# The last eight gate blocks of a hybrid attention block as seven block products for eight

## The chip, the cores and the metric

The kernel runs on one core of one Trainium2 chip. The metric is the device time of one execution in microseconds; the time before is the median of three runs. Engines: PE (TensorE, matmuls; PEld are its weight loads), DVE (VectorE), ACT (ScalarE), POOL (GpSimd), and SP (SyncE), which issues most DMAs. Each engine works through its own list of instructions in order and waits where an operand is not ready or a buffer is not free.

## The reference

One layer of a residual block with two attention branches, batch 1, sequence and model width 1024, all in float32. What matters here are the gates: the last 2048 columns of the input projection.

```python
h = rms_norm(x, g_pre_mix[l])
proj = h @ w_in[l]                      # 1024 x 5120
c0 = 3 * SB_WIDTH
c1 = c0 + 3 * DIFF_WIDTH
sb_q, sb_k, sb_v = jnp.split(proj[..., :c0], 3, axis=-1)
d_q, d_k, d_v = jnp.split(proj[..., c0:c1], 3, axis=-1)
gates = jax.nn.sigmoid(proj[..., c1:])
gate_sb, gate_diff = jnp.split(gates, N_BRANCHES, axis=-1)
y_sb = stick_breaking_attention(...)     # 8 heads of 64
y_diff = differential_attention(...)     # 4 heads, two softmax maps each
merged = gate_sb * (y_sb @ w_sb_out[l]) + gate_diff * (y_diff @ w_diff_out[l])
x = x + rms_norm(merged @ w_o[l], g_post_mix[l])
h = rms_norm(x, g_pre_mlp[l])
u = jnp.square(jax.nn.relu(h @ w_up[l]))
x = x + rms_norm(u @ w_down[l], g_post_mlp[l])
```

## The kernel before

Every product is taken in three float32r matmuls: each operand is split into a high part (a cast on ACT) and the rest (a subtraction on DVE), and high x high, high x low and low x high are added in one PSUM bank. `load_split` (L95 to L104) does this for a weight block: a DMA into a tile with tag raw (two buffers), the cast (L102), the subtraction (L103).

h, transposed, lies in eight tiles `h_hi[k]` and eight `h_lo[k]` of 128 x 1024: k counts 128 rows of the model width, the columns are the sequence. A gate block b (`gate`, L453, through `project`, L189) is 128 columns of the projection: for each half of the sequence it adds 24 matmuls of 128x512 (L196 to L198: eight k, three each) in a bank with tag acc, which has two; ACT copies the sum out (L456) and SP stores it in `gate_dram`. Gates are only needed by the next stage, mix (L542 to L582), where g is loaded back, passed through the sigmoid and multiplied.

The attention runs in eight units: four of two stick-breaking heads, then four differential heads. A unit's steps (j = 3, 1, 2, 0, a pair of query tiles each) go: scores z (PE L262, L263, in the two banks of tag sc), bias added and the row minimum found (DVE L389), exponential (ACT L394), the combination of the two maps (DVE L400 to L404), transposes (PE L281), their split (ACT L287, DVE L288), the products with v (PE L342 to L344), and a normalisation that goes back and forth between ACT, DVE and PE (L348 to L368, with ss on PE at L355 and L356). The steps of the last head, called head 3 below, begin when its bias rows have been loaded (L372); there is one bias buffer. Score tiles have the tags big_s (four buffers, j = 3 and 2) and small_s (four buffers, j = 1 and 0).

Gates 0 to 7 are written between the units' steps (`GATES`, `fill`). Gates 8 to 15 are written in a plain loop behind the last step (L530 to L532), but the order of the instructions on each engine is not the written one: a scheduler (the tile framework's, with a timeline of its own) lays them out when the kernel is built, with buffers of a tag handed on as they come free. It put much of these eight gates between the steps of heads 2 and 3.

The MLP behind it already uses seven block products for eight: `sums` (L724) forms sums of weight blocks on POOL, L817 to L830 form sums of h on DVE.

Of the kernel before, what the change touches and what calls it, by code (L numbers as in the profile page):

```python
# [9 lines left out]
F32 = mybir.dt.float32  # L10
F32R = mybir.dt.float32r
AF = mybir.ActivationFunctionType
ALU = mybir.AluOpType
# [3 lines left out]
P = 128  # L17
S = 1024
D = 1024
NK = D // P  # L20
NT = S // P
HALF = 512
# [19 lines left out]
def hybrid_block_kernel(  # L42
# [17 lines left out]
    nc = tc.nc  # L60
# [20 lines left out]
    def f32(ap):  # L81
        return ap.bitcast(F32)
# [46 lines left out]
    gate_dram = dram.tile([2 * NK, P, S], F32, name="gate_dram")  # L129
# [20 lines left out]
    with ExitStack() as actx:  # L150
        pa = actx.enter_context(tc.tile_pool(name="pa", bufs=2))

        h_hi = [big_tile(f"h_hi{k}") for k in range(NK)]
        h_lo = [big_tile(f"h_lo{k}") for k in range(NK)]
# [337 lines left out]
        qs, kh, kl, pair = [], [], [], []  # L492
# [34 lines left out]
            for _ in filler:  # L527
                pass
        waiting()
        for b in range(GATES[-1].stop, 2 * NK):  # L530
            for _ in gate(b):
                pass  # L532


        def load_gate(b, i):
# [7 lines left out]
        for u in range(N_SB + N_DIFF):  # L543
            if u < 6:
                tag = ("qs", "kh", "kl")[u % 3]
                parts = [pa.tile([P, S], F32R, tag=tag, name=f"y{u}_{p}", bufs=4) for p in range(2)]
            else:
                both = pa.tile([P, 2, S], F32R, tag="v", name=f"y{u}", bufs=3)
# [8 lines left out]
        for b in range(NK):  # L557
            w_hi, w_lo = load_split(w_mix[b], f"mix{b}")
            g = [load_gate(b, i) for i in range(2)]
            accs = [[any_tile(f"mix{b}_{i}_{c}") for c in range(2)] for i in range(2)]  # L560
            for k in range(NK):
                i, ks = k // 4, slice(k * P, (k + 1) * P)
                y_hi, y_lo = y[k]
                for st, mv, first, last in ((w_hi, y_hi, True, False), (w_hi, y_lo, False, False), (w_lo, y_hi, False, True)):
                    for c in range(2):
                        cs = slice(c * HALF, (c + 1) * HALF)
                        nc.tensor.matmul(  # L567
                            accs[i][c], st[:, ks], mv[:, cs],
                            start=(first and k % 4 == 0), stop=(last and k % 4 == 3),
                        )  # L570
            for c in range(2):
                cs = slice(c * HALF, (c + 1) * HALF)
# [178 lines left out]
    for t in range(NT):  # L751
# [337 lines left out]
```

## Time and profile before

| | us |
|---|---|
| median of three runs | 1463.02 (1461.43 to 1464.18) |
| the profiled execution | 1462.9 |
| its span, first to last instruction | 1461.2 |
| attention units, last gates among them, until the last gate matmul | to 653.5 |
| mix starts | 653.75 |
| DVE busy / ACT busy / POOL busy, of the span | 1018.6 / 742.9 / 320.6 |

Spans of one execution are read against the 1462.9, which lies 0.1 from the median. A line such as `0.69 DVE L389` is a start, a duration, an engine and a line of the kernel; what stands in square brackets is the idle time ahead of it and what ended it. Instructions on PE overlap: one 128x512 matmul lasts 0.39 us and the next starts 0.23 us after it.

### The profile page before, as it was taken

What the parts mean: (1) busy time and instruction counts of PE and PEld (TensorE: products, weight loads), DVE (VectorE), ACT (ScalarE), POOL (GpSimd) and SP (SyncE); (2) the same over time, 40 slices, a digit from 0 to 9 for tenths busy, and PEclk for the clock granted to TensorE, in tenths of its full rate; (3) what the DMA queues carried; (4) which work ended last, traced back from release to release, by engine and by line L of the source; (5) the groups of instructions that cost most, each with busy time, mean ns of one, the idle gap of its engine ahead of it and who ended that gap; (6) DMA issues with size and microseconds to landing.
All of it is one profiled execution on the core that took longest, in us unless ns stands there. A gap on an engine that the chain in (4) does not pass through costs nothing. (4 is left out here: it accounts for less than half of the span.)

```text
span 1461.2 us, 20068 instructions
## 1 busy us (share of the span) xinstructions
PE 1437.1 (98%) x7302; PEld 1221.7 (84%) x7302; DVE 1018.6 (70%) x1468; ACT 742.9 (51%) x1352; POOL 320.6 (22%) x312
## 2 busy tenths in 40 slices
PE   7999999999999999999999989999999999999997
PEld 6888898899889888888888868788888888888886
DVE  5477987898779876535555489766665669764783
ACT  6355766676556645753434454444444443534350
POOL 2022331231000000000002316333330357232611
PEclk9999999999999999999999999999999999999999
DMA  5242213221322245554347735544446785678681
GB/s 206 76 135 66 69 48 80 65 73 48 93 74 66 80 130 170 179 197 139 138 149 238 245 117 178 189 148 143 152 158 202 256 287 178 200 229 285 205 288 58
DMA packets 93946, 220.50 MB, mean 151 GB/s; under 512 B 9260, under 2 KB 24856, under 8 KB 93848
## 3 DMA queue, kind: packets, MB, share of 16 engines
q1 hardware_dynamic: 79448, 199.30, 42.5%
q10 hardware_dynamic: 14400, 19.93, 3.8%
q8 instruction: 57, 0.93, 0.3%
q14 instruction: 41, 0.34, 0.1%
HBM read 153.11 MB, written 60.05 MB: 146 GB/s over the span
## 5 line engine op out<-in xcount | busy, mean ns | idle before, releaser
L331 DVE TENSOR_TENSOR_SCAN rest<-rest 128x896 f32<-128x896 f32 (+3 forms) x64 | 87.7, 1374 | 20.7 <-POOL rest L326 20.3
L198 PE MATMUL acc_gate<-h_hi,lo_gate 128*128 128x512 f32 x256 | 101.0, 394 | 0.0
L196 PE MATMUL acc_gate<-h_hi,hi_gate 128*128 128x512 f32 x256 | 100.8, 394 | 0.0
L197 PE MATMUL acc_gate<-h_lo,hi_gate 128*128 128x512 f32 x256 | 100.7, 394 | 0.0
L608 DVE TENSOR_TENSOR lS_lo<-raw_S,lS_hi 128x1024 fp32r<-128x1024 f32 x32 | 53.8, 1680 | 39.8 <-ACT lS_hi L607 39.8
L326 POOL TENSOR_SCALAR_AFFINE_SELECT rest<-rest 128x128 f32<-128x128 f32 x64 | 23.6, 369 | 240.7 <-ACT rest L322 228.0
L957 PE MATMUL dS<-rT_hi,lS_hi 128*128 128x512 f32 x192 | 74.7, 389 | 0.0
L957 PE MATMUL dS<-rT_lo,lS_hi 128*128 128x512 f32 x192 | 74.7, 389 | 0.0
L957 PE MATMUL dS<-rT_hi,lS_lo 128*128 128x512 f32 x192 | 74.7, 389 | 0.0
L607 ACT CAST lS_hi<-raw_S 128x1024 fp32r<-128x1024 f32 x32 | 33.7, 1053 | 73.9 <-DMA raw_S<-s_dramS 43.5
L567 PE MATMUL mix<-y,hi_mix 128*128 128x512 f32 x256 | 68.6, 389 | 0.0
L394 ACT ACTIVATE s<-s,low 128x896 f32<-128x896 f32 (+7 forms) x64 | 49.7, 777 | 30.1 <-DVE low L389 29.9
L389 DVE CUSTOM_DVE_ANT_0 s<-z,bias 128x512 f32<-128x512 f32 (+3 forms) x64 | 37.0, 588 | 32.3 <-PE z L263 26.1
L567 PEld LDWEIGHTS mix<-y,hi_mix 128*128 128x128 f32 x256 | 48.1, 188 | 10.0
L198 PEld LDWEIGHTS acc_gate<-h_hi,lo_gate 128*128 128x128 f32 x256 | 48.2, 188 | 9.2
L197 PEld LDWEIGHTS acc_gate<-h_lo,hi_gate 128*128 128x128 f32 x256 | 48.2, 188 | 8.8
L196 PEld LDWEIGHTS acc_gate<-h_hi,hi_gate 128*128 128x128 f32 x256 | 48.2, 188 | 8.6
L326 POOL TENSOR_SCALAR_AFFINE_SELECT beta<-beta 128x128 f32<-128x128 f32 x64 | 54.0, 844 | 3.4 <-ACT beta L323 2.3
L287 ACT CAST wth_sb<-tr_sb 128x512 fp32r<-128x512 f32 (+1 forms) x80 | 41.2, 548 | 26.5 <-PE tr_sb L281 25.1
L116 POOL TENSOR_SCALAR rstd_o<-s 128x1 f32<-128x1 f32 x8 | 2.7, 342 | 235.8 <-DMA grow<-in_g_rows_dram 211.4
L288 DVE TENSOR_TENSOR wtl_sb<-tr_sb,wth_sb 128x512 fp32r<-128x512 f32 (+1 forms) x80 | 48.5, 628 | 7.7 <-ACT wth_sb L287 7.4
L322 ACT ACTIVATE rest<-z 128x512 f32<-128x512 f32 (+2 forms) x96 | 47.3, 492 | 9.2 <-PE z L263 7.8
(351 smaller groups left out, 4763.2 us busy)
## 6 DMA issues: line engine op xcount, KB each, us to landing
s_dramS<-us SPq DMA_DIRECT2D x64, 256.0 KB, 4.2
raw_S<-s_dramS SPq DMA_DIRECT2D x32, 512.0 KB, 4.5
s_dramA<-u ACTq DMA_DIRECT2D x48, 256.0 KB, 3.1
raw_A<-s_dramA SPq DMA_DIRECT2D x24, 512.0 KB, 4.1
raw_gate<-in_w_in_dram SPq DMA_DIRECT2D x16, 512.0 KB, 3.7
gate_dram<-gt SPq DMA_DIRECT2D x32, 256.0 KB, 2.5
y<-y_dram SPq DMA_DIRECT2D x16, 512.0 KB, 7.2
g<-gate_dram SPq DMA_DIRECT2D x16, 512.0 KB, 4.3
```

Of the source, the lines that this page charges most:

```text
L196: nc.tensor.matmul(acc, w_hi[:, ks], h_hi[k][:, cs], start=(k == 0), stop=False)
L197: nc.tensor.matmul(acc, w_hi[:, ks], h_lo[k][:, cs], start=False, stop=False)
L198: nc.tensor.matmul(acc, w_lo[:, ks], h_hi[k][:, cs], start=False, stop=(k == NK - 1))
L287: nc.scalar.copy(hi[:, :n], tr[:, :n])
L288: nc.vector.tensor_tensor(lo[:, :n], tr[:, :n], f32(hi[:, :n]), op=ALU.subtract)
L322: nc.scalar.activation(rest[:, c0:c1], z, AF.Sigmoid, scale=-1.0)
L326: nc.gpsimd.affine_select(tl[:, dg], tl[:, dg], pattern=[[-1, P]], compare_op=ALU.is_gt, fill=fill, base=0, channel_multiplier=1,)
L331: nc.vector.tensor_tensor_scan(back, back, back, 1.0, op0=ALU.mult, op1=ALU.bypass)
L394: e = nc.scalar.activation(s[:, :nk], s[:, :nk], AF.Exp, bias=low, scale=-1.0, accum_out=sums[:, m:m + 1],)
L567: nc.tensor.matmul(accs[i][c], st[:, ks], mv[:, cs], start=(first and k % 4 == 0), stop=(last and k % 4 == 3),)
L608: nc.vector.tensor_tensor(lo, raw, f32(hi), op=ALU.subtract)
L957: nc.tensor.matmul(acc, st[:, e, ts], mv[:, e, :], start=(first and e == 0 and i == 0), stop=(last and e == 1 and i == 2))
```

## The change

The loop over the last eight gates (8 to 15) is replaced. The gates go in four pairs (b0, b1). For a pair, the weights A (two column blocks by two halves of the model width) and h as four quarters B (half of the model width by half of the sequence, four k each) make a product of two by two blocks, which is done in seven block products of 12 matmuls each:

- B11, B22 and B21 are products with a quarter of h as it is. First all four pairs' B11, then B22, then B21. The factor of B22 is a sum of the pair's four weight blocks, formed by three sums on POOL (`gate_sums(n, 1)`); the others take a half block as loaded. The results of B11 and B22 are kept in four buffers of tag big_s.
- T1, T2, T3 and T4 are sums of quarters of h. They are formed on DVE, nine instructions and a cast for each of four k, into tiles of the attention's tags (v, qs, kl, yt) and then written over the quarters (T1 over B11's, T2 over B22's, T4 over B21's, T3 over B12's), each when the products that read the quarter are done.
- The last sixteen products take these. Per pair: P6 with T2, P5 with T1, P7 with T3, P4 with T4, in banks of tags sc, av, tr and acc. Their weights are loaded again, two sums of them are formed on POOL (three instructions, `gate_sums(n, 2)`), four splits follow, and six additions on DVE make the four results.

All raw loads go through the same two raw buffers as before.

```diff
-        for b in range(GATES[-1].stop, 2 * NK):
-            for _ in gate(b):
-                pass
+        C0, C1 = slice(0, HALF), slice(HALF, S)
+        gate_pairs = [(b, b + 1) for b in range(GATES[-1].stop, 2 * NK, 2)]
+        def quarter(j, cs):
+            return [(h_hi[4 * j + k][:, cs], h_lo[4 * j + k][:, cs]) for k in range(4)]
+        quarters = {"T1": quarter(0, C0), "T3": quarter(0, C1), "T4": quarter(1, C0), "T2": quarter(1, C1)}
+        PLACE = {"B11": "T1", "B12": "T3", "B21": "T4", "B22": "T2"}
+        def gate_product(acc, w, name):
+            w_hi, w_lo = w
+            for k, (hi, lo) in enumerate(quarters[PLACE.get(name, name)]):
+                ks = slice(k * P, (k + 1) * P)
+                for i, (st, mv) in enumerate(((w_hi, hi), (w_hi, lo), (w_lo, hi))):
+                    nc.tensor.matmul(acc, st[:, ks], mv, start=(k == 0 and i == 0), stop=(k == 3 and i == 2))
+        def split_w(src, name):
+            both = stream.tile([P, 2, HALF], F32R, tag="w", name=f"gw_{name}", bufs=4)
+            nc.scalar.copy(both[:, 0, :], src)
+            nc.vector.tensor_tensor(both[:, 1, :], src, f32(both[:, 0, :]), op=ALU.subtract)
+            return both[:, 0, :], both[:, 1, :]
+        def raw_gate(b, cs, name):
+            raw = stream.tile([P, S], F32, tag="raw", name=f"raw_{name}")
+            nc.sync.dma_start(out=raw[:, cs], in_=w_in[GATE + b][:, cs])
+            return raw
+        def gate_sums(n, part):
+            f0, f1 = (raw_gate(b, slice(0, S), f"g{part}_{b}") for b in gate_pairs[n])
+            a11, a12, a21, a22 = (f[:, cs] for f in (f0, f1) for cs in (C0, C1))
+            s1 = pa.tile([P, HALF], F32, tag="small_s", name=f"gs1_{part}_{n}", bufs=4)
+            nc.gpsimd.tensor_tensor(s1, a21, a22, op=ALU.add)
+            if part == 2:
+                nc.gpsimd.tensor_tensor(a21, a11, a21, op=ALU.subtract)
+            nc.gpsimd.tensor_tensor(a11, s1, a11, op=ALU.subtract)
+            if part == 1:
+                nc.gpsimd.tensor_tensor(a12, a12, a11, op=ALU.subtract)
+            return s1, f0, f1
...
+        t1 = pa.tile([P, 4, HALF], F32, tag="v", name="gt1", bufs=3)
+        t2, t4 = ([pa.tile([P, 2, HALF], F32, tag=tag, name=f"g{tag}{i}", bufs=4) for i in range(2)] for tag in ("qs", "kl"))
+        for k in range(4):
+            (a_hi, a_lo), (b_hi, b_lo), (c_hi, c_lo), (d_hi, d_lo) = (quarters[t][k] for t in ("T1", "T3", "T4", "T2"))
+            t1k, t2k, t4k = t1[:, k, :], t2[k // 2][:, k % 2, :], t4[k // 2][:, k % 2, :]
+            r = pa.tile([P, HALF], F32, tag="yt", name=f"gr_{k}")
+            nc.vector.tensor_tensor(r, f32(b_hi), f32(b_lo), op=ALU.add)
+            nc.vector.tensor_tensor(t1k, r, f32(a_hi), op=ALU.subtract)
+            nc.vector.tensor_tensor(t1k, t1k, f32(a_lo), op=ALU.subtract)
+            nc.vector.tensor_tensor(t2k, f32(d_hi), f32(d_lo), op=ALU.add)
+            nc.vector.tensor_tensor(r, t2k, r, op=ALU.subtract)
+            nc.scalar.copy(b_hi, r)
+            nc.vector.tensor_tensor(b_lo, r, f32(b_hi), op=ALU.subtract)
+            nc.vector.tensor_tensor(t2k, t2k, t1k, op=ALU.subtract)
+            nc.vector.tensor_tensor(t4k, f32(c_hi), t2k, op=ALU.subtract)
+            nc.vector.tensor_tensor(t4k, t4k, f32(c_lo), op=ALU.add)
+        p1s, p3s = ([pa.tile([P, 2, HALF], F32, tag="big_s", name=f"gp{p}_{i}", bufs=4) for i in range(2)] for p in (1, 3))
...
+        for name, cs in (("B11", C0), ("B22", C1), ("B21", C1)):
+            for n, (b0, b1) in enumerate(gate_pairs):
+                if name == "B22":
+                    src = gate_sums(n, 1)[1]
+                else:
+                    src = raw_gate(b0, cs, f"g{name}_{b0}")
+                acc = acc_tile(f"gate_{name}_{n}")
+                gate_product(acc, split_w(src[:, cs], f"{name}_{n}"), name)
...
+            where, tiles = {"B11": ("T1", None), "B22": ("T2", t2), "B21": ("T4", t4)}[name]
+            for k, (hi, lo) in enumerate(quarters[where]):
+                src = t1[:, k, :] if tiles is None else tiles[k // 2][:, k % 2, :]
+                nc.scalar.copy(hi, src)
+                nc.vector.tensor_tensor(lo, src, f32(hi), op=ALU.subtract)
+        for n, (b0, b1) in enumerate(gate_pairs):
+            s1, f0, f1 = gate_sums(n, 2)
+            w2 = split_w(f0[:, C0], f"s2_{n}")
...
+            gate_product(p6, w2, "T2")
+            nc.vector.tensor_tensor(p1, p6, p1, op=ALU.add)
+            gate_product(p5, w1, "T1")
...
+            gate_product(p7, w3, "T3")
...
+            gate_product(p4, w22, "T4")
```

The scheduler lays out the whole again. Three places show what became of the order; the numbers in names are buffers or counters, z are scores, tr transposes, avd products with v, ss the sum of squares, acc_gate and gate_B the gates' banks, gw their split weights, raw_g the pairs' weights as loaded.

PE, behind the second score tiles of head 3, before:

```order
L262 MATMUL z_0_7_0_6542<-kh_dfk_0_5974,qs_dfq_0_5908 128x512
L263 MATMUL z_0_7_0_6542<-kl_dfk_0_5976,qs_dfq_0_5908 128x512
L198 MATMUL acc_gate_0_7051<-h_hi_162,lo_gate_7048 128x512
L196 MATMUL acc_gate_1_7079<-h_hi_155,hi_gate_7047 128x512
L262 MATMUL z_0_7_512_6547<-kh_dfk_0_5974,qs_dfq_0_5908 128x512
L263 MATMUL z_0_7_512_6547<-kl_dfk_0_5976,qs_dfq_0_5908 128x512
L197 MATMUL acc_gate_1_7079<-h_lo_163,hi_gate_7047 128x512
L198 MATMUL acc_gate_1_7079<-h_hi_155,lo_gate_7048 128x512
L196 MATMUL acc_gate_1_7079<-h_hi_156,hi_gate_7047 128x512
L197 MATMUL acc_gate_1_7079<-h_lo_164,hi_gate_7047 128x512
```

PE at the same place in the changed kernel:

```order
L262 MATMUL z_0_7_0_6542<-kh_dfk_0_5974,qs_dfq_0_5908 128x512
L263 MATMUL z_0_7_0_6542<-kl_dfk_0_5976,qs_dfq_0_5908 128x512
L356 MATMUL ss_2_6494<-sqp_2_6491,ones 128x256
L262 MATMUL z_0_7_512_6547<-kh_dfk_0_5974,qs_dfq_0_5908 128x512
L263 MATMUL z_0_7_512_6547<-kl_dfk_0_5976,qs_dfq_0_5908 128x512
L262 MATMUL z_1_7_0_6554<-kh_dfk_1_5975,qs_dfq_1_5909 128x512
L263 MATMUL z_1_7_0_6554<-kl_dfk_1_5977,qs_dfq_1_5909 128x512
L262 MATMUL z_1_7_512_6559<-kh_dfk_1_5975,qs_dfq_1_5909 128x512
L263 MATMUL z_1_7_512_6559<-kl_dfk_1_5977,qs_dfq_1_5909 128x512
L262 MATMUL z_0_2_0_6609<-kh_dfk_0_5974,qs_dfq_0_5908 128x384
```

Where gate matmuls lay between the scores, one score now stands behind the other: two B11 products come earlier, the other products later.

DVE, the end of head 3's last normalisation, before:

```order
L361 TENSOR_TENSOR sq_0_6961<-sq_0_6961,r_0_6962 128x256
L362 SCALAR_TENSOR_TENSOR w_0_6963<-sq_0_6961,r_0_6962 128x256
L363 SCALAR_TENSOR_TENSOR w_0_6963<-w_0_6963,r_0_6962 128x256
L364 SCALAR_TENSOR_TENSOR y_0_6960<-y_0_6960,subln,w_0_6963 128x256
L367 TENSOR_TENSOR yp_0_6979<-y_0_6960,yp_0_6979 128x256
L103 TENSOR_TENSOR lo_mix_7590<-raw_mix_7587,hi_mix_7589 128x1024
L578 TENSOR_TENSOR g_0_7515<-mix_0_0_7521,g_0_7515 128x512
```

DVE at the same place in the changed kernel (gr, gt and gqs are the sums of h; gw_B_2 is the split for the third B22 product):

```order
L362 SCALAR_TENSOR_TENSOR w_0_6963<-sq_0_6961,r_0_6962 128x256
L551 TENSOR_TENSOR gw_B_2_7179<-raw_g_12_7170,gw_B_2_7179 128x512
L363 SCALAR_TENSOR_TENSOR w_0_6963<-w_0_6963,r_0_6962 128x256
L364 SCALAR_TENSOR_TENSOR y_0_6960<-y_0_6960,subln,w_0_6963 128x256
L581 TENSOR_TENSOR gr_6988<-h_hi_155,h_lo_163 128x512
L367 TENSOR_TENSOR yp_0_6979<-y_0_6960,yp_0_6979 128x256
L582 TENSOR_TENSOR gt_6983<-gr_6988,h_hi_155 128x512
L583 TENSOR_TENSOR gt_6983<-gt_6983,h_lo_163 128x512
L585 TENSOR_TENSOR gr_6988<-gqs_6984,gr_6988 128x512
L588 TENSOR_TENSOR gqs_6984<-gqs_6984,gt_6983 128x512
```

The first two of the B22 splits stand ahead of this piece, the third in it, the fourth some ten rows behind it; the sums of h, but for four of the 36, and all twelve rewrites follow the attention, where mix followed.

SP, the loads around head 3's bias, before:

```order
L98 DMA raw_gate_7169<-in_w_in_dram 128x1024
L551 DMA y_0_7483<-y_dram_79 128x1024
L551 DMA y_0_7479<-y_dram_78 128x1024
L551 DMA y_1_7480<-y_dram_78 128x1024
L551 DMA y_1_7484<-y_dram_79 128x1024
L372 DMA bias_6508<-bias_rows 128x1024
L551 DMA y_0_7487<-y_dram_80 128x1024
L551 DMA y_1_7488<-y_dram_80 128x1024
```

SP at the same place in the changed kernel (y are the attention's results, loaded for mix; raw_g_10 and raw_g_11 the weights of the second pair):

```order
L556 DMA raw_g_8_7120<-in_w_in_dram 128x1024
L556 DMA raw_g_9_7122<-in_w_in_dram 128x1024
L658 DMA y_0_7656<-y_dram_79 128x1024
L658 DMA y_1_7657<-y_dram_79 128x1024
L372 DMA bias_6508<-bias_rows 128x1024
L368 DMA y_dram_84<-yp_1_6308 256x1x256
L368 DMA y_dram_84<-yp_2_6504 256x1x256
L368 DMA y_dram_84<-yp_0_6603 256x1x256
L658 DMA y_0_7668<-y_dram_82 128x1024
L658 DMA y_0_7652<-y_dram_78 128x1024
L658 DMA y_1_7669<-y_dram_82 128x1024
L658 DMA y_1_7653<-y_dram_78 128x1024
```

Ahead of the bias two gate loads and two y loads now stand in place of one gate load and four y loads; the next row is the load of raw_g_10, behind four y loads.

More of the change, by code (lines that the diff above doesn't have):

```diff
@@ new lines, in store_gate @@
+        def store_gate(b, cs, tile_):
+            nc.sync.dma_start(out=gate_dram[b, :, cs], in_=tile_)
+        t1 = pa.tile([P, 4, HALF], F32, tag="v", name="gt1", bufs=3)
[14 more added lines that the diff above has]
+            nc.vector.tensor_tensor(t4k, t4k, f32(c_lo), op=ALU.add)
@@ new lines, in hybrid_block_kernel, with kept @@
+        p1s, p3s = ([pa.tile([P, 2, HALF], F32, tag="big_s", name=f"gp{p}_{i}", bufs=4) for i in range(2)] for p in (1, 3))
+        def kept(tiles, n):
+            return tiles[n // 2][:, n % 2, :]
+        for name, cs in (("B11", C0), ("B22", C1), ("B21", C1)):
[6 more added lines that the diff above has]
+                gate_product(acc, split_w(src[:, cs], f"{name}_{n}"), name)
+                if name == "B21":
+                    c11 = pa.tile([P, HALF], F32, tag="small_s", name=f"gc11_{n}", bufs=4)
+                    nc.vector.tensor_tensor(c11, acc, kept(p1s, n), op=ALU.add)
+                    store_gate(b0, C0, c11)
+                else:
+                    nc.scalar.copy(kept(p1s if name == "B11" else p3s, n), acc)
+            where, tiles = {"B11": ("T1", None), "B22": ("T2", t2), "B21": ("T4", t4)}[name]
[3 more added lines that the diff above has]
+                nc.vector.tensor_tensor(lo, src, f32(hi), op=ALU.subtract)
```

15 lines of the change are left out of this document (added).

## The prediction

> **What bounds the kernel now.** I read the page's busy shares first, then the stretch that the change touches: busy time in windows, the matmul timeline at its end, VectorE's timeline at its beginning. The columns of a window row are its length, then PE, PEld, DVE, ACT and POOL busy time with instruction counts, the granted clock, the DMA share and GB/s.
>
> ```profile
> span 1461.2 us, 20068 instructions
> PE 1437.1 (98%) x7302; PEld 1221.7 (84%) x7302; DVE 1018.6 (70%) x1468; ACT 742.9 (51%) x1352; POOL 320.6 (22%) x312
> ...
> 540.00:560.00 20.00, 20.00 (x108) 17.10 (x107) 9.78 (x30) 9.42 (x25) 0.15 (x1) 1.00 0.76 250
> 560.00:580.00 20.00, 20.00 (x96) 16.73 (x95) 17.23 (x44) 11.10 (x24) 0.00 (x0) 1.00 0.35 119
> ...
> 640.00:660.00 20.00, 20.00 (x91) 16.57 (x90) 6.60 (x12) 7.84 (x11) 0.00 (x0) 1.00 0.54 185
> ...
> 555.40:653.60 98.20, 98.20 (x498) 83.22 (x497) 56.18 (x140) 63.06 (x113) 0.12 (x1) 1.00 0.50 165
> ...
> 653.52 0.39 PE L198 MATMUL acc_gate<-h_hi,lo_gate 128*128 128x512 f32 x1
> 653.75 0.84 PE L567 MATMUL mix<-y,hi_mix 128*128 128x512 f32 x3
> ```
>
> PE has no idle time at all from 540 us to the last gate matmul at 653.52 us; the next stage (mix) starts at 653.75. But it is full only because the last eight gates, which need nothing from the attention, are laid between the attention's short matmuls. VectorE, at 56.18 of 98.20 us, shows the room there is. The last head (head 3 of the differential attention) starts when its bias has landed:
>
> ```profile
> 555.37 0.69 DVE L389 CUSTOM_DVE_ANT_0 s<-z,bias 128x512 f32<-128x512 f32 x1 [5.93 <-DMA bias<-bias_rows]
> ...
> 612.50 0.42 DVE L389 CUSTOM_DVE_ANT_0 s<-z,bias 128x256 f32<-128x256 f32 x1 [0.48 <-PE z L263]
> ```
>
> VectorE sat 5.93 us for that load, and reached the last scores of the head at 612.50. PE covered both with gates. So the question is not what a product costs but whether PE still has something to do while VectorE works.
>
> **The change, part by part.** Prices of single instructions:
>
> ```profile
> 939.43 2.72 PE c L781 x12
> ...
> 667.32 0.68 DVE L580 TENSOR_TENSOR g<-g,g 128x512 f32<-128x512 f32 x1
> 667.92 1.46 DVE L582 TENSOR_TENSOR m_lo<-g,m_hi 128x512 fp32r<-128x512 f32 x2
> ...
> L581 ACT CAST m_hi<-g 128x512 fp32r<-128x512 f32 x10 | 6.2, 624 | 10.1 <-DVE g L580 10.1
> ...
> L735 POOL TENSOR_TENSOR s<-up x8: 1285/1290/1890, 866.7 to 1087.5; 128x512 f32<-128x512 f32 x8
> ...
> raw_gate<-in_w_in_dram SPq DMA_DIRECT2D x16, 512.0 KB, 3.7
> ...
> y<-y_dram SPq DMA_DIRECT2D x16, 512.0 KB, 7.2
> ...
> L103 DVE TENSOR_TENSOR lo_gate<-raw_gate,hi_gate 128x1024 fp32r<-128x1024 f32 x6 | 7.3, 1222 | 4.3 <-ACT hi_gate L102 4.3
> ...
> L103 DVE TENSOR_TENSOR lo_mix<-raw_mix,hi_mix 128x1024 fp32r<-128x1024 f32 x1 | 1.2, 1227 | 0.5 <-ACT hi_mix L102 0.5
> ...
> L361 DVE TENSOR_TENSOR sq<-sq,r 128x256 f32<-128x256 f32 x6 | 2.5, 424 | 7.0 <-ACT r L360 7.0
> ```
>
> A product of 12 matmuls takes PE 2.72 us. VectorE starts the next instruction 0.60 us after a 128x512 one (667.32 to 667.92). A 128x512 cast is 0.62 on ACT, a 128x512 sum 1.29 on POOL, a 512 KB gate load lands in 3.7.
>
> Removed: 32 products become 28, so 48 matmuls or 4 x 2.72 = 10.9 us of PE. Also eight wide splits (1.22 on VectorE each) and 16 evictions on ACT, which no chain waits for.
>
> Added: 104 instructions of 128x512 on VectorE (28 splits of weights, 36 sums of h, 12 rewrites of its quarters, 28 combinations; the order has 96 rows more, eight wide splits being gone): 104 x 0.60 = 62 us against 8 x 1.22 = 10 us. 24 sums on POOL, 31 us on an engine that idles here; 17 more DMAs on SP. On ACT casts take the place of evictions; it was busy 63.06 of 98.20 us, and only its casts ahead of splits lie on a chain. None of this is long for its engine over the whole kernel. What matters is where it stands.
>
> Step 1, head 3 without cover. By the order, PE had 201 gate matmuls between head 3's first and last scores, and 361 from its first scores to the end of the gates; now it has 24 between those scores. The first two B11 products are spent before head 3; the other two wait for score tiles to come free (their kept results go into tag big_s). So while the bias lands PE stands (no loss in itself, since VectorE waits for the same load at the same time: I cost the start at nothing, with 3 us either way for the two 512 KB loads that now go ahead of it in place of two others), and then VectorE sets the pace. Its attention work after 555.4 is 56.18 less the splits, 7.3 + 1.2: 47.7 us. Two late normalisations of seven instructions at 0.42 (5.9 us) come afterwards, so 41.8 us plus some 1.5 of waits (estimate): the head's main part is over at about 598.7, where VectorE does the first B22 split. That is sooner than before, and PE idles for most of it.
>
> Step 2, the B22 rounds. The four B22 products need a load, three sums on POOL, a cast and a split, in two raw buffers. The next pair's load can only start when the last split has freed its buffer: 3.7 + 3 x 1.29 + 0.62 + 0.60 + 0.4 for the hand-overs = 9.2 us a round, against 2.72 us of product. On SP the second pair's load also stands behind four y loads, which wait for head 3's last scores and take 7.2 to land: from about 592 that gives the same 603 as the buffer does. So splits at 598.7, 607.9, 617.1, 626.3. They stand in VectorE's queue ahead of, and among, the sums of h, so VectorE waits with them: the late normalisations and twelve sums fit between, no more.
>
> Step 3, the sums of h. After the fourth B22 split the order has 37 more VectorE instructions before the first product of the last set (P5) has all it needs: 37 x 0.60 = 22.2, 648.5. PE has four B21 products (10.9 us) to do meanwhile and idles for the rest.
>
> Step 4, the last sixteen products: 16 x 2.72 = 43.5, less 1.4 for the six matmuls sent ahead, plus 0.5 of waits: 691.1. Their loads and sums (9.2 us) fit under the 10.9 us that a pair takes, ten VectorE instructions (6 us) too, so PE sets the pace.
>
> Step 5, the clock. What an idle PE costs afterwards is shown where the MLP starts:
>
> ```profile
> 844.70:847.80 3.10, 0.47 (x3) 0.04 (x1) 2.26 (x3) 0.00 (x0) 0.00 (x0) 0.99 0.06 25
> 847.80:849.40 1.60, 1.56 (x8) 1.59 (x9) 1.60 (x3) 0.00 (x0) 0.00 (x0) 0.50 0.52 105
> 849.40:851.30 1.90, 1.90 (x7) 1.57 (x6) 1.86 (x4) 0.97 (x2) 0.00 (x0) 0.54 0.70 226
> 851.30:853.30 2.00, 2.00 (x10) 1.62 (x9) 2.00 (x4) 2.00 (x6) 0.00 (x0) 1.00 0.62 229
> ```
>
> After 2.6 us without a matmul the granted clock is 0.50 to 0.54 for 3.5 us, then 1.00 again: half of 3.5, or 1.7 us, when the last products start. 692.8.
>
> The Trainium skill (TensorE: Matmul & The Clock Gate, What's actually happening) has the PE clock at half after an idle window of about 3.4 us and back after as long of sustained work. The trace agrees on the size of the penalty, and shows it after a shorter gap.
>
> The sum: mix starts at 692.8 instead of 653.75, 39 us later; behind it nothing is changed. The profiled execution took 1462.9 (1.7 around its span of 1461.2), the median of the three runs is 1463.0: 1502.
>
> **The rivals.**
> - VectorE never waits (1488). If the rounds hide wholly, VectorE needs 47.7 + 53 x 0.60 = 79.5 us from 555.4 until P5: 634.9, then 42.6 and 1.7: mix at 679.2, 25 us later. This is the floor of this order. For it: the first pair's loads stand ready early, and VectorE may fall behind the rounds by itself; against it, the 9.2 us of a round, three times.
> - Head 3 keeps its old pace (1522). Its last scores then come at 612.5 instead of about 592, and the rounds, whose y loads wait for them, move by 20. POOL's sums at their maximum of 1.89 would add 3 x 3 x 0.6 = 5 to the forecast, which also lies inside. For it: ACT and VectorE alternate in each step; against: then each score matmul stood among gates.
> - Half clock throughout (1514). If PE stays cold in the starved stretch, head 3's 16 pairs of score matmuls (0.46 each at full clock) and as much again of transposes and products with v take twice as long on VectorE's chain, some 12 to 15 us with little cover: 12 taken. The clock rule cited above would give this, if gaps come often enough.
> - Faster (1452). All of the added work is hidden and 10.9 us are won. The point from which it decides: after 555.4 PE has 98.2 - 361 x 0.227 = 16 us of attention and 120 matmuls (27 us) of early products, so it runs dry at 599; to win anything, P5 must start within 10.9 us of that, by 610. VectorE has 47.7 us of attention to do by then, so the 53 instructions before P5 would have to cost 0.13 us each and not 0.60.
> - No change needs the same at 0.2 to 0.25 us each.
>
> **How the numbers follow.** Forecast 0.56, VectorE's floor 0.18, old pace 0.10, half clock 0.08, faster 0.06, no change 0.02. Within 0.2%, some 3 us, is what the runs can tell from no change. So slower 0.92, same 0.02, faster 0.06. The range goes from the floor less the 3 us of the bias load, 1485, to the old pace and 2 us of slower sums, 1524.
>
> **What would show it.** Right: PE idle of 40 us or more between 549 and 690 in the windows, where there was none; VectorE over 80% busy from 556 to 600; the B22 splits about 9 us apart, waiting for a cast that waits for POOL, whose first sum waits for a load; granted clock near 0.5 in pieces; P5 releasing at about 648 on VectorE; the last sixteen products in 43 us; mix at about 693, and everything after it as long as before. Wrong: PE without gaps in 556 to 600 would mean that the products were available after all; splits 5 us apart, that the raw buffers are not the bound; a mix start before 679, that my price of 0.60 or the order's count is off.

## The result, and the profile after

The changed kernel takes 1516.1 us (median; 1514.0 to 1518.2) against 1462.8 for the kernel before on the same chip: 53.3 us more, ratio 1.0356, 95% interval 1.0339 to 1.0373. The forecast was 1502, range 1485 to 1524. The direction came as forecast, and PE starves at the places that were named; the loss is 14 us larger than the sum.

The profiled execution took 1518.15 (its span 1516.4). It is 3.7 us late already at the first scores of the differential heads (354.1 instead of 350.4), ahead of anything that the change moves; head 3's wait for its bias takes that back (1.67 us of it instead of 5.93). Mix starts at 710.79 instead of 653.75, 57.0 us later (one matmul of mix stood at 648.09 before). Some 2 us come back behind mix.

The first two lines of the page, and the stretch in windows (columns as above): from the first idle of PE to the end of head 3's main part, to the point where the first of the last products has its operands, and to the last of them.

```profile
span 1516.4 us, 20192 instructions
PE 1453.5 (96%) x7254; PEld 1225.1 (81%) x7254; DVE 1090.8 (72%) x1564; ACT 741.1 (49%) x1369; POOL 353.0 (23%) x336
...
549.00:600.00 51.00, 38.34 (x187) 29.75 (x187) 44.00 (x125) 28.71 (x71) 4.06 (x4) 0.82 0.28 96
600.00:661.00 61.00, 38.06 (x133) 28.23 (x132) 51.50 (x77) 23.70 (x47) 17.28 (x12) 0.75 0.56 183
661.00:711.00 50.00, 45.52 (x190) 36.09 (x189) 30.99 (x43) 12.87 (x18) 12.55 (x9) 0.97 0.55 175
```

PE, which had no idle time here, now has 12.7, 22.9 and 4.5 us of it, 40 in all, and works at a mean granted clock of 0.82 and 0.75 in the first two pieces. VectorE is busy 86% of the first and 84% of the second.

The B22 rounds, as VectorE's splits, and as the first of POOL's three sums in each round, with what POOL waited for:

```profile
600.05 0.68 DVE L551 TENSOR_TENSOR gw_B<-raw_g,gw_B 128x512 fp32r<-128x512 f32 x1
611.07 0.69 DVE L551 TENSOR_TENSOR gw_B<-raw_g,gw_B 128x512 fp32r<-128x512 f32 x1
622.93 0.69 DVE L551 TENSOR_TENSOR gw_B<-raw_g,gw_B 128x512 fp32r<-128x512 f32 x1
635.43 0.68 DVE L551 TENSOR_TENSOR gw_B<-raw_g,gw_B 128x512 fp32r<-128x512 f32 x1
...
594.19 1.26 POOL L563 TENSOR_TENSOR gs<-raw_g 128x512 f32<-128x512 f32 x1 [38.22 <-DVE s L404]
604.44 1.40 POOL L563 TENSOR_TENSOR gs<-raw_g 128x512 f32<-128x512 f32 x1 [6.18 <-DMA raw_g<-in_w_in_dram]
615.51 1.53 POOL L563 TENSOR_TENSOR gs<-raw_g 128x512 f32<-128x512 f32 x1 [6.87 <-DMA raw_g<-in_w_in_dram]
...
682.07 1.29 POOL L563 TENSOR_TENSOR gs<-raw_g 128x512 f32<-128x512 f32 x1 [9.02 <-DMA raw_g<-in_w_in_dram]
696.95 1.26 POOL L563 TENSOR_TENSOR gs<-raw_g 128x512 f32<-128x512 f32 x1 [10.54 <-DMA raw_g<-in_w_in_dram]
```

The first split comes at 600.05; then rounds of 11.0, 11.9 and 12.5 us. What POOL waits for is only a part of a round; the rest is taken apart below, under step 2. The last two rows are from the last products: there too a pair waits for its load. That POOL's first sum waits 38 us for `s` is the score tile (tag small_s) that holds its result.

VectorE at the first of the last products, and PE at its last two pairs and at the start of mix:

```profile
658.04 1.75 DVE L615 TENSOR_TENSOR h_lo<-gt,h_hi 128x512 fp32r<-128x512 f32 x1
660.31 0.68 DVE L622 TENSOR_TENSOR gwt_lo<-gs,gwt_hi 128x512 fp32r<-128x512 f32 x1
...
684.06 0.50 PE L546 MATMUL gav<-h_hi,gwt_hi 128*128 128x512 f32 x1 [0.64 <-ACT gwt_hi L621]
698.92 0.50 PE L546 MATMUL gav<-h_hi,gwt_hi 128*128 128x512 f32 x1 [2.82 <-ACT gwt_hi L621]
710.79 1.52 PE L674 MATMUL mix<-y,hi_mix 128*128 128x512 f32 x6
```

P5 of the first pair has all it needs at 661.0, when its low weights are written.

### The profile page after: what moved, and what is told of

The parts are those of the page before. It is cut to its first block, busy times and chain, and to the rows that moved or that the text cites. A ratio compares the mean times of both kernels' runs of the same rounds, so it can differ in the third digit from the quotient of the medians.

```text
span 1516.4 us, 20192 instructions
## 1 busy us (share of the span) xinstructions
PE 1453.5 (96%) x7254; PEld 1225.1 (81%) x7254; DVE 1090.8 (72%) x1564; ACT 741.1 (49%) x1369; POOL 353.0 (23%) x336
## 3 DMA queue, kind: packets, MB, share of 16 engines
q1 hardware_dynamic: 81752, 205.59, 42.6%
## 4 chain that ended last, share of the span: by engine, by line
PE 80%; DVE 9%; issue 4%; DMA 3%; ACT 2%; POOL 2%; SPq 0%; DVEq 0%; POOLq 0%; ACTq 0%
PE dS L1064 11%; PE dA L1064 9%; PE mix L674 6%; PE c L888 4%; PE p_av L888 4%; PE p_tr L888 4%; PE o L763 4%; PE z L262 2%; PE p_sc L888 2%; PE z L263 2%; PE acc_gate L196 2%; PE acc_gate L197 2%; PE acc_gate L198 2%; PE tr_sb L281 2%; PE av L301 1%
## 5 line engine op out<-in xcount | busy, mean ns | idle before, releaser
L331 DVE TENSOR_TENSOR_SCAN rest<-rest 128x896 f32<-128x896 f32 (+3 forms) x64 | 87.6, 1373 | 22.2 <-POOL rest L326 21.9
L322 ACT ACTIVATE rest<-z 128x512 f32<-128x512 f32 (+2 forms) x96 | 47.2, 492 | 10.8 <-PE z L263 9.7
L888 PE MATMUL c<-hB_hi,wa_hi 128*128 128x512 f32 x128 | 50.1, 393 | 2.3 <-ACT p L973 1.1
L198 PE MATMUL acc_gate<-h_hi,lo_gate 128*128 128x512 f32 x128 | 50.5, 394 | 0.0
L197 PE MATMUL acc_gate<-h_lo,hi_gate 128*128 128x512 f32 x128 | 50.5, 394 | 0.0
L196 PE MATMUL acc_gate<-h_hi,hi_gate 128*128 128x512 f32 x128 | 50.4, 394 | 0.0
L888 PE MATMUL c<-hB_lo,wa_hi 128*128 128x512 f32 x128 | 49.9, 390 | 0.0
L888 PE MATMUL c<-hB_hi,wa_lo 128*128 128x512 f32 x128 | 49.8, 389 | 0.0
L1064 PE MATMUL dA<-rB_hi,lA_hi 128*128 128x512 f32 x128 | 49.8, 389 | 0.0
```

The lines of the kernel that those rows point to most:

```text
L196: nc.tensor.matmul(acc, w_hi[:, ks], h_hi[k][:, cs], start=(k == 0), stop=False)
L197: nc.tensor.matmul(acc, w_hi[:, ks], h_lo[k][:, cs], start=False, stop=False)
L198: nc.tensor.matmul(acc, w_lo[:, ks], h_hi[k][:, cs], start=False, stop=(k == NK - 1))
L331: nc.vector.tensor_tensor_scan(back, back, back, 1.0, op0=ALU.mult, op1=ALU.bypass)
L888: nc.tensor.matmul(acc, st[:, ks], mv, start=(first and k == 0 and i == 0), stop=(k == 3 and i == 2), skip_group_check=True,)
L1064: nc.tensor.matmul(acc, st[:, e, ts], mv[:, e, :], start=(first and e == 0 and i == 0), stop=(last and e == 1 and i == 2))
```

## The experiments

Theory A: the change fails by its order. It takes from PE the work that needed nothing from VectorE and lay under head 3, and gives it products that wait for sums, rounds of loads and casts. Rival B: the added work on VectorE and POOL is itself the price. Each run below is compared with runs of the kernel before on its own chip; the differences are between medians.

| run | us | against before | ratio, 95% | last gate matmul (before: 653.5) |
|---|---|---|---|---|
| the change | 1516.1 | +53.3 | 1.0356 (1.0339 to 1.0373) | 710.6 |
| e1_behind | 1512.1 | +47.2 | 1.0333 (1.0315 to 1.0352) | 702.7 |
| e2_eighth_out | 1455.1 | −9.9 | 0.9939 (0.9923 to 0.9954) | 645.3 |
| e4_no_hsums | 1507.3 | +42.3 | 1.0289 (1.0273 to 1.0306) | 698.4 |
| e6_no_wsums | 1491.5 | +26.5 | 1.0181 (1.0164 to 1.0198) | 683.4 |
| e7_no_sums | 1473.8 | +10.4 | 1.0068 (1.0053 to 1.0083) | 661.5 |
| e3_raw_kh | 1509.9 | +46.5 | 1.0316 (1.0297 to 1.0335) | 703.2 |
| e5b_dve_kh | 1504.5 | +41.1 | 1.0285 (1.0247 to 1.0323) | 696.2 |
| e8_hyb4 | 1495.1 | +31.7 | 1.0216 (1.0196 to 1.0236) | 684.0 |
| f2_noyt_dvekh | 1502.7 | +38.0 | 1.0254 (1.0232 to 1.0276) | 693.3 |
| f3_hyb4_noyt_dvekh | 1488.1 | +23.4 | 1.0154 (1.0133 to 1.0176) | 674.3 |
| g1_before_hsums | 1463.1 | −0.9 | 0.9991 (0.9978 to 1.0005) | 655.8 |
| g2_before_wsums | 1464.3 | +0.3 | 1.0001 (0.9991 to 1.0011) | 654.6 |

**e1_behind: the old gates, without covering.**

```diff
-                    nc.tensor.matmul(acc, w_hi[:, ks], h_hi[k][:, cs], start=(k == 0), stop=False)
+                    first = nc.tensor.matmul(acc, w_hi[:, ks], h_hi[k][:, cs], start=(k == 0), stop=False)
+                    if late[0] and k == 0:      # gates 8 to 15
+                        after(first, last_matmul[0])   # head 3's last ss matmul
```

> The kernel before, all sixteen matmuls-chains of gates 8 to 15 on PE laid behind head 3's last matmul; nothing else changed, no block products. Theory A (the loss is first of all lost cover): head 3 runs alone from 555.8, ends about 608 as it did in the changed kernel, then 16 chains of 24 matmuls x 0.227 = 87 us and 1.7 us of low clock: mix at about 697 instead of 653.75, total about 1506. Rival B (lost cover is worth little, the block products' own sums make the loss): head 3 gains about as much speed as the gates lose, total under 1475. Rival C (head 3 keeps its old pace when alone, last scores at 612): mix at about 715, total about 1524.

1512.1, 6 over theory A's number. If all eight gates stand behind head 3, with no block product and no sum, the lost cover costs 47 us. That is nearly the size of the whole loss, but not a measure of what the change loses by its order, which e7 below shows. The 6 us are head 3's tail. Alone, its normalisations go one after the other, and PE waits for each; the last two of these waits:

```profile
605.00 0.58 PE L357 MATMUL ss<-sqp,ones 128*128 128x256 f32 x1 [5.28 <-ACT sqp L354]
612.40 0.58 PE L357 MATMUL ss<-sqp,ones 128*128 128x256 f32 x1 [5.33 <-ACT sqp L354]
```

**e2_eighth_out: what the saved matmuls are worth.** One k of eight is left out of gates 8 to 15 (`for k in range(n)` with n = 7 there).

> The kernel before with the last of the eight k left out of each chain of gates 8 to 15: 48 matmuls fewer, which is what the change saves, and no sums in exchange (part of the product is missing from these gates). Theory A (PE is full from 540 to 653, so its work is the price there): 48 x 0.227 = 10.9 us less, 1452. Rival (VectorE's chain through head 3 sets the end as soon as PE has less to do): no gain, 1463, with PE idle in 600 to 643.

9.9 us less, of the 10.9 (95%: 6.7 to 11.3). That is about the most the change could have won. PE is idle for 1.5 us at 620 to 640, where it was full before.

**e4_no_hsums, e6_no_wsums, e7_no_sums: leave out the sums.** e4 drops the loop that forms t1, t2 and t4 and the writes over the quarters; e6 drops POOL's additions:

```diff
-            s1 = pa.tile([P, HALF], F32, tag="small_s", name=f"gs1_{part}_{n}", bufs=4)
-            nc.gpsimd.tensor_tensor(s1, a21, a22, op=ALU.add)
...
-            return s1, f0, f1
+            return a12, f0, f1
```

e7 drops both.

> The changed kernel without the sums of h and without writing them over the quarters (the last sixteen products take the plain quarters, so eight gates come out different): 52 DVE instructions and 16 casts fewer. Theory A (the rounds of load, three sums on POOL and split go on at 11 to 12 us, four for B22 and four for the last products, and the sums of h are only part of the loss): first of the last products at about 645 instead of 660, mix at about 695 instead of 711, total about 1500. Rival B (the 100% busy VectorE of 630 to 660 is the loss): mix by 675, total 1480 or less. Rival C (rounds alone are the bound): unchanged, 1514 or more. If sums on POOL lengthen because VectorE works at the same time, they go down from 1.4 to 1.6 us to 1.3 here.

> The changed kernel without the sums of weight blocks (the loads stay, the halves as loaded take the place of the sums, so eight gates come out different): no POOL instruction in this stretch. Theory A (rounds of 11 to 12 us are mostly POOL's): rounds of about 6.6 (5 load, 0.62 cast, 0.60 split, 0.4), B22's splits through by 620, first of the last products at about 642, PE's own pace of 43.5 us behind that, mix at about 687 instead of 711, total about 1491. Theory A also has the VectorE instructions of 580 to 640 back at 0.42 us for 128x256 and 0.68 for 128x512, since their doubling came from POOL working at the same time. Rival B (VectorE's sums of h bound it alone): total 1508 or more. Rival C (the load, not POOL, is the long part of a round): rounds stay at 9 us or more, 1500 to 1508.

> The changed kernel with neither the sums of weight blocks nor the sums of h (loads, splits and all 28 products stay, on unsummed operands, so eight gates come out different). What is left of the change is the order: products that come too late to lie under head 3, against 48 matmuls fewer. Theory A: PE is dry from 556 to about 590 but for two products, and then has 24 products, 24 x 2.72 = 65 us, at its own pace: mix at 660 to 668, total 1468 to 1476. So even without any sum the change would not win its 10.9 us. Rival B (the sums are the whole loss): 1452 to 1458. Rival C (the loads alone, two raw buffers, hold the products up): mix at 675 or later, total 1483 or more.

e7 came out in its range, e4 7 us over (it has 48 VectorE instructions fewer, 1516 for 1564, and not the 52 of the expectation). e6 came out at its number, but not by its path, so the number is luck: B22's splits were through at 594.0 and not 620, the first of the last products began at 630.3 and not 642, and the products then waited for the sums of h, 53 us until mix and not PE's own 43.5. POOL's additions in e4's B22 rounds are back at 1.3 us, and VectorE's instructions in e6 at 0.42 and 0.68, as expected. Counted from e7 (+10.4), the sums of h alone cost 16 us (e6), the sums of weights alone 32 (e4), both together 43 (the change). They do not quite add (48 against 43, at the edge of what the intervals tell): VectorE works at the sums of h while the rounds go on. In e4 first, then in e6 (600 to 630, 630 to 660), in windows:

```profile
600.00:630.00 30.00, 17.21 (x56) 13.40 (x55) 14.70 (x26) 10.09 (x23) 11.59 (x9) 0.70 0.38 116
...
600.00:630.00 30.00, 19.06 (x88) 15.43 (x88) 19.83 (x40) 13.08 (x31) 0.00 (x0) 0.89 0.58 181
630.00:660.00 30.00, 25.31 (x89) 18.04 (x90) 29.96 (x51) 11.75 (x20) 0.00 (x0) 0.88 0.49 150
```

In e4 nobody is full at 600 to 630: VectorE 14.7 of 30 us, POOL 11.6, PE 17.2. That is a chain of waits, the rounds. In e6 VectorE is full from 630 to 660, first of all with the sums of h. Neither loss needs the other. What is left in e7 is the order alone: 10.4 us of loss although 48 matmuls are saved, which were worth 9.9 in e2, so some 20 us of lost cover.

**e3_raw_kh and e5b_dve_kh: shorter rounds.** e3 gives the loads four buffers; e5b also forms the weights' sums on DVE (`nc.vector` for `nc.gpsimd` in `gate_sums`).

```diff
-            f0, f1 = (raw_gate(b, slice(0, S), f"g{part}_{b}") for b in gate_pairs[n])
+            f0 = raw_gate(gate_pairs[n][0], slice(0, S), f"g{part}_{gate_pairs[n][0]}")
+            f1 = pa.tile([P, S], F32, tag="kh", name=f"gk{part}_{n}", bufs=4)
+            nc.sync.dma_start(out=f1, in_=w_in[GATE + gate_pairs[n][1]])
```

> The changed kernel with the second block of each pair loaded into a tile of tag kh (four buffers) instead of the second raw buffer, so two pairs of loads can be under way instead of one; the bias of head 3 then stands behind four gate loads on SP's queue instead of two. Theory A (a round of 11 to 12 us is long because the next load waits for the last split): B22's rounds go down to POOL's 3 x 1.45 and hand-overs, 5 us: splits through by 618 instead of 635, first of the last products at about 643, their rounds of 10 to 15 us hidden, mix at about 687, total about 1492, up to 1497 if the bias comes later. Rival B (the buffers do not matter, VectorE's sums of h are late by themselves): 1508 or more.

> As the run with kh tiles, and the 24 sums of weight blocks on DVE instead of POOL. Theory A (VectorE's instructions double in length while POOL adds, and POOL takes 1.3 to 1.6 us where VectorE takes 0.68): the 12 sums ahead of the first of the last products cost VectorE 12 x 0.60 = 7 us, the doubling goes (the 20 us of VectorE's busy time over the forecast), rounds end at 2.5 us each: mix at about 684, total about 1489, some us below the run with kh tiles alone. Rival B (no doubling by POOL, VectorE is simply full): 24 x 0.60 = 14 us more work on it, slower than the run with kh tiles by 7 us or more, 1499.

Both miss: 1509.9 for 1492, 1504.5 for 1489. The B22 splits of e3 did come early (604, 607, 613, 617 instead of 600 to 635), so the raw buffers were what set the round. But most of the gain was given back at the next wait. With buffers to spare, POOL's sums for the last products run beside VectorE's sums of h. In e3 a window there, and one POOL addition; in e5b, where POOL is out of it, a window:

```profile
640.00:650.00 10.00, 2.22 (x5) 0.62 (x3) 10.00 (x8) 1.33 (x3) 8.70 (x6) 0.50 0.16 61
...
657.84 11.24 POOL L567 TENSOR_TENSOR gk<-raw_g,gk 128x512 f32<-128x512 f32 x1 [9.14 <-DMA raw_g<-in_w_in_dram]
...
630.00:640.00 10.00, 0.00 (x0) 0.00 (x0) 10.00 (x19) 3.11 (x7) 0.00 (x0) 0.63 0.51 131
```

With POOL adding, VectorE issues 8 instructions in 10 us; without it, 19. In e5b VectorE is full, with sums of weights, splits and the first sums of h, and PE has no matmul at all for 10 us. The intervals of the two runs overlap, so it is not shown which of the two engines does the sums of weights at less cost here.

**f2_noyt_dvekh: the sums of h earlier.** In these runs the first sum of h through the intermediate r comes just ahead of head 3's last yp (624.4 and 625.0 in the change, 635.2 and 635.8 in e5b); both have tiles of tag yt. f2 is e5b with r kept in t4's tile:

```diff
-            r = pa.tile([P, HALF], F32, tag="yt", name=f"gr_{k}")
-            nc.vector.tensor_tensor(r, f32(b_hi), f32(b_lo), op=ALU.add)
+            nc.vector.tensor_tensor(t4k, f32(b_hi), f32(b_lo), op=ALU.add)
```

> As the run with kh tiles and the sums of weight blocks on DVE, and the intermediate r of the sums of h kept in t4's tile instead of a tile of tag yt (two buffers, which head 3's normalisations hold until 621 to 636: in every run so far the first sum of h begins within 7 us of the last yp). All sums of h then stand ahead of head 3's last scores in VectorE's list, 20 of them inside the head. Theory A (the sums of h are late because of that tag, and cost their 25 us behind the head because nothing else is left then): head 3 is longer by 20 x 0.60 = 12 us, but nothing stands between B21 and the last products: PE has 24 products, 65 us, from about 612 on: mix at about 678, total about 1488, 16 us below the run without this edit. Rival B (VectorE has the same work in all, so it only moves from behind the head into it): 1500 to 1505.

The tag was the cause of the late place: without it all sums of h stand ahead of head 3's last scores. The time hardly moves (+38.0 against +41.1, within the intervals), so rival B holds for this step. The wait only changes its place:

```profile
550.00:590.00 40.00, 24.57 (x75) 15.32 (x74) 40.00 (x101) 17.66 (x40) 0.14 (x1) 0.57 0.06 20
```

VectorE is full for 40 us, now with head 3 and the sums together, and PE, with little of its own, stands at a clock of 0.57.

**e8_hyb4 and f3_hyb4_noyt_dvekh: half the gates plain.** Gates 8 to 11 as before, two pairs by block products; f3 with f2's three edits as well, as the best version that the runs so far pointed to.

> Gates 8 to 11 as plain gates again, only 12 to 15 in two pairs by block products (24 matmuls saved instead of 48); everything else as changed. Theory A (the loss is first of all the cover of head 3): four plain gates, 192 matmuls or 43.5 us, lie under head 3, PE is full until about 605 to 615; then two B22 rounds and the sums of h (37 x 0.60 = 22 us, as many as for four pairs) stand open, and 8 products of 22 us follow: mix at about 672, total about 1481, a third of the loss. Rival B (loss in proportion to the pairs): half of it, about 1490. Rival C (with cover the sums hide): 5.4 us won, 1457.

> Gates 8 to 11 plain, 12 to 15 in two pairs by block products, with kh tiles for the second loads, the sums of weight blocks on DVE, and the sums of h in t4's tile instead of tag yt: the attempt at a version that wins. 24 matmuls fewer than before are 5.4 us, so no less than 1457.6. Theory A (with cover under head 3, sums that need no yt buffer and no rounds, only 12 products of 33 us are left when head 3 is through at 605 to 612): PE idle of 5 to 10 us in all, mix at 650 to 658, total 1459 to 1467, no difference or a little over. Rival B (VectorE, with 20 sums of h in head 3, becomes the bound of the head and holds PE): last scores at 620 or later, mix at 665, total 1475. Rival C (the two pairs' sums cost as much as in the run with four plain gates and nothing else): 1490.

Neither wins, and both are over theory A's numbers (1495 for 1481, 1488 for 1459 to 1467). e8 lies above even its rival B's 1490, and f3 close to its rival C's 1490. In e8 PE is full until 610 and then, from 620 to 680, idle for 21 of 60 us: as many sums of h as for four pairs, ahead of the last eight products. f3 in windows, under head 3 and after it:

```profile
550.00:600.00 50.00, 50.00 (x246) 42.18 (x245) 43.31 (x100) 23.46 (x49) 0.15 (x1) 1.00 0.26 87
600.00:675.00 75.00, 58.13 (x260) 47.52 (x259) 57.49 (x128) 42.72 (x83) 0.00 (x0) 0.84 0.67 221
```

Four plain gates are enough cover until 600, and head 3's sums and scores keep VectorE busy for 43 of 50 us under it. Then PE runs dry: 17 us of idle time and a clock of 0.84 for the rest. 5.4 us of saved matmuls do not pay for that. Which of the waits after 600 is the largest in f3 was not tried apart. No version with block products here beats the kernel before.

**g1_before_hsums and g2_before_wsums: the added work under full cover.** g1 adds 40 additions to the kernel before, on DVE, on the same operands; g2 adds 24 on POOL:

```diff
+            for op in (ALU.add, ALU.subtract, ALU.add):
+                nc.gpsimd.tensor_tensor(raw[:, 0:HALF], raw[:, 0:HALF], raw[:, HALF:S], op=op)
```

> The kernel before, all eight gates plain and in their old places, with 40 additions of 128x512 on DVE added (the sums of h, into tiles that nothing reads; none needs a tile of tag yt, all stand ahead of head 3's last scores): the VectorE work of the change under full cover. Theory A (extra work costs because it ends behind the cover, not as work): 24 us more on VectorE, last scores of head 3 at up to 636 instead of 612, PE has 160 matmuls or 36 us behind them, so at most a few us come out at the end: 1463 to 1470. Rival B (VectorE is the bound of the stretch, its work counts as such): plus 17 to 24 us, 1480 to 1487.

> The kernel before with three additions of 128x512 on POOL for each of gates 8 to 15, 24 in all as in the change, on the raw weights after their split (the result is not used, the raw buffer stays taken until they are done); gates plain and nearly in their old places. Theory A: VectorE's instructions double in length while POOL adds (24 x 1.4 = 34 us of POOL, so some 20 us more busy time on VectorE in the stretch, and single 128x256 instructions at 1.2 to 1.4 us), the raw buffer's round grows from 5 to 9 us against 10.9 us of matmuls of a gate, and PE stays covered: 1463 to 1468. Rival B (rounds with POOL in them cannot feed PE even when each carries 48 matmuls): PE idle between gates, plus 10 us or more. Rival C (POOL does not touch VectorE): VectorE's busy time as before, 56 us in 555 to 653.

Both cost nothing (0.9991 and 1.0001). The same stretch in g1, and in g2:

```profile
555.40:653.60 98.20, 98.20 (x501) 83.23 (x500) 70.17 (x166) 58.46 (x106) 0.00 (x0) 1.00 0.52 172
...
555.40:653.60 98.20, 98.19 (x496) 82.80 (x495) 61.91 (x140) 63.64 (x113) 24.13 (x18) 1.00 0.48 163
```

PE is as full as before. In g1 VectorE has 14 us more in this window (25.6 in all, 1044.2 against 1018.6), its last scores come at 629 instead of 612.5, and PE does not wait for them. So the work itself is free while PE has matmuls that do not depend on it. In the change 53 VectorE instructions stand ahead of products that PE needs next. The two kinds of sums were added to the kernel before one at a time; both together were not tried.

So neither theory is the whole. The order alone costs some 20 us against the 10 that it saves (e7, e2). The other 43 come with the sums, which cost nothing where no product waits for them (g1, g2) and here hold back the products that PE needs next.

## Why the prediction was right, and where it was short

- **Step 1 was right.** First B22 split 600.05, forecast 598.7; head 3's first scores at 555.83, forecast 555.4; VectorE was 89% busy from 556 to 600, where over 80% was named. PE's idle time from 549 to 690 is 36.8 us, a little under the 40 that were named; it is 40 to the end of the gates at 711.
- **Step 2 is the term that was mis-sized.** Its rounds were to take 9.2 us and took 11.0, 11.9 and 12.5; the fourth split came at 635.4, not 626.3. Of the 9.1 us, 1.4 are the later start and 7.7 the rounds. The load is not the cause: from the end of a split to the next pair's first addition on POOL it took 3.7 us in all three rounds (600.73 to 604.44, 611.76 to 615.51, 623.62 to 627.35), as priced. POOL's three additions took 4.2, 4.3 and 4.6 us and not 3.87, 1.5 us in all. The rest, 6.0 us, lies between POOL's last addition and the split. I had put one cast there and 0.4 for the hand-overs, which no row showed, 1.0 in sum; it took 2.4, 3.1 and 3.5. Round by round, POOL's last addition and what then held the cast or the split:

```profile
607.32 1.33 POOL L568 TENSOR_TENSOR raw_g<-raw_g 128x512 f32<-128x512 f32 x1
608.96 0.40 ACT L366 CAST yp<-y 128x256 fp32r<-128x256 f32 x1 [2.60 <-DVE y L364]
610.42 0.61 ACT L550 CAST gw_B<-raw_g 128x512 fp32r<-128x512 f32 x1
...
618.47 1.35 POOL L568 TENSOR_TENSOR raw_g<-raw_g 128x512 f32<-128x512 f32 x1
621.23 0.42 ACT L359 ACTIVATE r<-sq 128x256 f32<-128x256 f32 x1 [2.69 <-DVE sq L358]
622.00 0.60 ACT L550 CAST gw_B<-raw_g 128x512 fp32r<-128x512 f32 x1
...
630.36 1.59 POOL L568 TENSOR_TENSOR raw_g<-raw_g 128x512 f32<-128x512 f32 x1
631.98 0.62 ACT L550 CAST gw_B<-raw_g 128x512 fp32r<-128x512 f32 x1 [3.50 <-POOL raw_g L568]
634.83 0.68 DVE L582 TENSOR_TENSOR gt<-gr,h_hi 128x512 f32<-128x512 f32 x1
```

  In the first two rounds the cast stands in ACT's list behind steps of head 3's normalisation, and these wait for VectorE. In the third the cast comes at once, and the split stands in VectorE's list behind sums of h (the last of them at 634.83, the split at 635.43). A short instruction waits for whatever stands ahead of it in its engine's list.
- **Step 3 was right.** 37 VectorE instructions were to stand between the fourth split and P5's last operand; the trace has 37 between 635.43 and 660.31. They took 25.6 us and not 22.2: three of the last ones ran beside POOL (1.15, 1.76 and 1.75 instead of 0.68).
- **Step 4 failed.** I let PE set the pace of the last sixteen products because a round of 9.2 us fits under 10.9. But POOL's first additions for the four pairs start at 654.44, 668.70, 682.07 and 696.95, 13.4 to 14.9 us apart. Here the buffers come free only after three casts and three splits (3.6 to 4.8 us behind POOL, where I had put 1.2), and the loads are slower: 4.5 and 5.2 us for the second and third pair; the fourth pair's last one was issued at 689.99, when the third pair's last split ended, and POOL starts 7.0 later. One addition and a cast later PE begins the pair's first product. So the first products of the last three pairs start at 672.3, 684.06 and 698.92, 11.8 and 14.9 us apart. 661.0 to 710.8 is 49.8 us; forecast 42.6 and 1.7 for the clock.
- **Step 5** put one cold start of 1.7 us at the end. The granted clock was at 0.82 and 0.75 for 112 us. In the last stretch, where PE has the most to do, it is 0.97 of 50 us, 1.5 us, as forecast in size. Head 3 was not slowed by it: its last scores come at 592.2, forecast about 592, where the rival of half clock throughout asked for 12 us more. What the low clock costs between 600 and 661 was not tried apart.
- **Not priced at all: POOL against VectorE.** The change and e6 have the same 1564 VectorE instructions, and 1090.8 against 1068.0 us of busy time. Most of the 22.8 us come from POOL working beside it; two runs with the same VectorE and POOL work (before and e1) differ by 3.9. They lie inside the terms above.
- **The sum:** 39 forecast, 1.4 later start, 7.7 rounds, 3.4 sums, 5.5 last products: 57.0, the shift of mix in the trace. That 1516 still lies in the range is in part luck: its upper end was drawn for a head 3 at its old pace, which did not come, and not for these waits.
- **The faster rival** asked that P5 start by 610. It started at 661. (The 361 matmuls in that working count from PE's own first scores at 548.1; from 555.4 on there are 339, which moves the point from 610 to 615. And P5 at that point would be no change and not yet a win, so the 0.2 to 0.25 us of the last rival do not go with the 0.13 of this one.) Even without any sum (e7) the kernel is 10.4 us slower, so no price of a sum would have saved this order.

## What to carry to other kernels

Before saving matmuls on a full PE, ask what the saved ones were covering: matmuls that depend on nothing fill another stage's waits, and replacing them by products that come later costs the fill: some 20 us here for a gain of 10 at most. The sums, which held the products back, cost 43 more. Price the hand-overs of a chain by what stands ahead in each engine's list, not by the instruction's own length. Look at which buffers the new work borrows: score tiles and a tag of two decided its place more than its length did, and freeing one wait only showed the next. Extra work on another engine was free as long as PE had other matmuls (g1, g2), and cost much of its length where PE waited for it (32 us for 34 us of additions on POOL).

## What the runs showed of the hardware

VectorE and POOL stand in each other's way, instruction by instruction. In the changed kernel, the same instruction with POOL adding beside it and without, one that takes two tiles from SBUF while POOL adds, and one whose first operand lies in PSUM, also beside POOL:

```profile
604.73 1.39 DVE L362 SCALAR_TENSOR_TENSOR w<-sq,r 128x256 f32<-128x256 f32 x1
614.50 0.42 DVE L362 SCALAR_TENSOR_TENSOR w<-sq,r 128x256 f32<-128x256 f32 x1
627.38 1.78 DVE L588 TENSOR_TENSOR gqs<-gqs,gt 128x512 f32<-128x512 f32 x1
654.69 0.68 DVE L607 TENSOR_TENSOR gc<-gate_B,gp 128x512 f32<-128x512 f32 x1
```

1.39 instead of 0.42, and 1.78 instead of 0.68, are the instruction's own time and about what is left of an addition on POOL. The one that reads PSUM keeps its 0.68. The other way round a POOL addition took 11.24 us instead of 1.3 in e3 (657.84 to 669.08), while VectorE ran 16 instructions back to back that take both operands from SBUF. It came to its end when VectorE had reached two that read PSUM:

```profile
667.84 1.27 DVE L632 TENSOR_TENSOR gp<-gav,gp 128x512 f32<-128x512 f32 x2
```

Why the two engines take turns at 640 to 650 in e3 and not here is open. The Trainium skill (SBUF — State Buffer, SBUF: two separate sides) says that VectorE with two SBUF inputs and GpSimd lock a shared pair of ports for a whole instruction, and that the other blocks; these rows agree. In g2, 24 additions on POOL made only 8.6 us more busy time on VectorE (1027.2 against 1018.6 over the whole span), less than half of what I expected. That fits head 3's instructions that read PSUM, and was not tried apart.
